# Layer 0 of a two-layer encoder trunk: row-normed inputs, evacuation on ScalarE, the residual as transposing matmuls, rotation tables as outer products

## The chip, the cores and the metric

One core of a Trainium2 chip runs the whole program. The metric is the device time of one execution in microseconds (us); the median of several runs is given.

## What is computed

Two sequences (512 and 256 tokens, each with 16 meta tokens ahead: 528 + 272 = 800 columns) go through two layers:

```python
h = concat(meta, x)                                  # 800 tokens x 1024 features
for l in range(2):
    hn = rms_norm(h, norm_mix[l])
    xa, ga, xq, xi, xff, xfb, xg, xu = split(hn @ w_in[l])
    ya = rglru(xa, ga)                               # 384 wide: conv, gates, scan both ways, gelu gate
    yb = hgrn2(silu(xq), xi, xff, xfb) * silu(xg)    # 384 wide: chunked decay attention, both ways
    yc = s5(xu)                                      # 256 wide: state space scan both ways, gelu, glu
    ym = concat(rms_norm(ya), rms_norm(yb), rms_norm(yc)) * mix_gain[l]
    h = h + ym @ w_out[l]
    h = h + relu(rms_norm(h, norm_mlp[l]) @ w_up[l])**2 @ w_down[l]
y = rms_norm(h[:, 16:], norm_final)
```

## The kernel before

Features lie on the partitions, the 800 tokens along the free dimension. A large product splits both operands into two float32r parts and runs three passes, x high by w high (L434), x low by w high (L435) and x high by w low (L436), for each of 8 (or 3, or 2) tiles of 128 input features, and for the tokens in two halves of 400. One half of one output tile fills one PSUM bank of the pool `mm`, which has three; `hb` has three and `rb` two, for everything else. Weights arrive as raw tiles `wr` (three buffers), ScalarE rounds them to `wh` (L419) and GpSimd takes the rest `wl` (L420).

A scheduler lays out the order of each engine at build time from priorities; `ORDERS` lists the steps of the mixing part of a layer (`ri`, `rc`: RG-LRU, `hi`, `hc`: HGRN2, `si`, `sc`: S5, one per tile of 128 features; `sf`: the glu of S5; `gr`, `gh`, `gw`, `hf`: smaller steps; `fB`, `fA`, `fC`: `finish`, the normed operands of `w_out` of the HGRN2, RG-LRU and S5 groups). Each engine runs its list in order, SyncE (SP), which issues the loads, too.

The functions that the change touches:

- `load` (L275) brings in seven tiles of rows of the input, sums their squares (ScalarE, L305), transposes them on TensorE (L313), rounds them to operands `xh` (ScalarE, L317) and `xl` (VectorE, L318), and copies them as the residual `h` (L319), which goes to DRAM. The rows are not normed; 1/rms of each token becomes a tile `r1` by matmuls (L306).
- Evacuations of `w_in`'s products therefore multiply by `r1` on VectorE: `scaled` (L464), `rglru_in` (L488). `hgrn_in` then takes a tanh of all 800 tokens on ScalarE (L549).
- `s5_setup` (L706) builds the tables of S5 in DRAM, for layer 0 beside the first steps, for layer 1 beside layer 0's MLP. For four sets (direction, group of four) the rotation table of 4 x 100 complex numbers is doubled seven times, six VectorE operations (L726 to L731) each: lengths 1, 2, 4, ... 64, then 36.
- `s5` (L879) handles a feature tile in four blocks: loads (L901 to L907), matmuls (L913), scans, matmuls (L940, L943) and at the end transposes (L950). `s5_glu` (L955) runs eight matmuls (L966).
- `finish` (L993), with `LT` = 1 for layer 0: the group that comes first (fB) is scaled before the product, the second (fA) and third (fC) after it.
- `mix_out` (L1066) runs `w_out` in three parts for layer 0, one per group (fB: 3 input tiles, fA: 3, fC: 2), 16 halves each. Part 0 adds the residual, loaded back from DRAM (L1091), as it leaves PSUM (L1095); parts 1 and 2 multiply (L1098) and add (L1099).
- `mlp` (L1104): evacuations of `w_up` are a relu on ScalarE (L1123) and a product on VectorE (L1124).

Of the kernel before, what the change touches and what calls it, by code (L numbers as in the profile page):

```python
# [24 lines left out]
D = 1024  # L25
# [18 lines left out]
# order in which the parts of a layer's mixers are issued  # L44
# [4 lines left out]
HALVES = ((0, 400, 0), (400, 400, 400))  # L49
HALVES_LAST = ((16, 512, 0), (544, 256, 512))  # L50
# [12 lines left out]
# per layer: what is moved in the issue order, pools of SBUF in their order, tiles of rs, hd, hs and ra, parts that  # L63
# take their tiles elsewhere, outputs that stay on chip, groups merged in w_out's first pass, engines
# [3 lines left out]
IO, PAD = ['x', 'm', 'p', 'h', 't'], 5600  # L68
# [5 lines left out]
AP = [0, 0]  # L74

class Trunk:
# [52 lines left out]
    def setup(self):  # L129
# [16 lines left out]
        # level masks: the highest bit in which s and t differ  # L146
# [12 lines left out]
        # scores of a chunk pair, block-diagonal: the blocks beside the diagonal stay zero  # L159
# [4 lines left out]
        # what leaves the chip for a while  # L164
# [19 lines left out]
        # s5 skip gains: (g2 h) rows, (l gp) columns  # L184
# [6 lines left out]
        # s5 step sizes over the states  # L191
# [9 lines left out]
        # lower bounds: softmax over the depth, running sum less the first  # L201
# [13 lines left out]
        # forget gate = hA*t + hB, key/2 = -hK*t + hK, with t = tanh(x/2)  # L215
# [6 lines left out]
        # rg-lru: softplus(-lambda) with log1p by its atanh series  # L222
# [23 lines left out]
    def gate_weights(self, l):  # L246
        """Block-diagonal gates: (i, d, r|i)."""
# [27 lines left out]
    def load(self):  # L275
        """The residual and the operands of the first w_in, half by half of the tokens."""
        nc = self.nc
        src = [(self.ins["meta_tokens"], 16)]
        src += [(self.ins["x_prompt"][0, i * 128 : i * 128 + 128], 128) for i in range(4)]
        src += [(self.ins["x_sample"][0, i * 128 : i * 128 + 128], 128) for i in range(2)]  # L280
        xs = []
        for a, n in src:
# [7 lines left out]
        h = [self.t("h") for _ in range(KD)]  # L290
        self.x = [(self._t(self.op, (128, T), F32R, f"xh{k}", 1), self._t(self.op, (128, T), F32R, f"xl{k}", 1)) for k in range(KD)]
        stat = [self.ps("hb") for _ in range(2)]
        sq = self.c((128, 8), "sq")
        for b, parts in enumerate(((0, 1, 2, 3), (4, 0, 5, 6))):
            sl = slice(b * 400, b * 400 + 400)
            # the tokens' sums of squares, from the partitions to the free dimension
# [3 lines left out]
            o = 0  # L300
            for i in parts:
                x, n = xs[i]
                if b == 0 or i:
                    junk = self.t("m", (n, D))
                    nc.scalar.activation(junk[:], x[:], AF.Square, accum_out=sq[0:n, i : i + 1])  # L305
                nc.tensor.matmul(stat[b][:, o : o + n], ap(sq[0:n], i, [[0, 128]]), self.ident[0:n, 0:n], start=True, stop=True)  # L306
                o += n
            for k in range(KD):
# [63 lines left out]
    def split(self, k, y, gain, rs=None, n=T):  # L372
        """Operand k = y*gain (*rs) as two float32r parts that add up to it exactly."""
# [12 lines left out]
    def sumsq(self, ys, n=T):  # L386
        """The sum of squares over the partitions of all tiles, on every partition: two PSUM halves."""
# [38 lines left out]
    def product(self, w, xs, halves, evac):  # L426
# [14 lines left out]
    def fetch(self, name, l, c):  # L441
        """128 columns of a weight matrix of 1024 rows, split."""
# [8 lines left out]
    def project(self, l, cols, evacs):  # L451
        """Columns of w_in, 128 from each of cols."""
# [24 lines left out]
    def rglru_in(self, l, i):  # L477
# [7 lines left out]
        def ev(b, ps):  # L485
            for c0, n in (((0, 400),), ((400, 128), (528, 272)))[b]:
                o = c0 + (2 if c0 < 528 else 5)
                nc.vector.tensor_tensor(out=xp[:, o : o + n], in0=ps[:, c0 - 400 * b : c0 - 400 * b + n], in1=self.r1[:, c0 : c0 + n], op=MULT)  # L488
# [53 lines left out]
    def hgrn_in(self, l, i):  # L542
        nc = self.nc
        FP, K2, Q, V = self.t("hd", (128, 2, T)), self.t("hd", (128, 2, T)), self.s(), self.s()
        self.project(l, (XFF + 128 * i, XFB + 128 * i), [self.scaled(K2[:, d]) for d in range(2)])
        for d in range(2):
            c = (d * 2 + l) * 3 + i
            col = lambda x: x[:, c : c + 1]
            nc.scalar.activation(K2[:, d], K2[:, d], AF.Tanh, scale=0.5)  # L549
            nc.vector.tensor_scalar(out=FP[:, d], in0=K2[:, d], scalar1=col(self.hA), scalar2=col(self.hB), op0=MULT, op1=ADD)  # L550
            nc.vector.tensor_scalar(out=K2[:, d], in0=K2[:, d], scalar1=col(self.hN), scalar2=col(self.hK), op0=MULT, op1=ADD)
        tq = self.s()
        self.project(l, (XQ + 128 * i, XI + 128 * i), (self.scaled(Q), self.scaled(V)))
        nc.scalar.activation(tq[:], Q[:], AF.Tanh, scale=0.5)
        nc.vector.scalar_tensor_tensor(out=Q[:], in0=tq[:], scalar=1.0, in1=Q[:], op0=ADD, op1=MULT)
# [18 lines left out]
    def scores(self, K, Q, P, Pm, m):  # L574
        """Scores [s, t] of level m, chunk by chunk, into the places where it applies."""
# [659 lines left out]
```

## Time and profile before

| | us |
|---|---|
| median of 3 runs (lowest to highest) | 2202.79 (2199.93 to 2209.05) |
| profiled execution: its span, first to last instruction | 2201.6 |
| TensorE matmuls busy (PE) | 2087.4 |
| VectorE busy (DVE) | 1118.9 |
| ScalarE busy (ACT) | 753.8 |
| GpSimd busy (POOL) | 811.9 |

The profiled execution has no time of its own beside its span. The page names engines PE (TensorE matmuls), PEld (weight loads), DVE, ACT, POOL (GpSimd) and SP (SyncE). Times inside the program are us from its start. PEclk is the granted clock of TensorE, 1.00 being its full speed. Layer 0's mixing part runs from 0 to about 557 us, its MLP to about 1190 us.

### The profile page before, as it was taken

Reading aid. Unit: us, or ns where it says so; the run is one execution under the profiler, and the core shown is the slowest. Engines: PE = TensorE matmul, PEld = TensorE weight load, DVE = VectorE, ACT = ScalarE, POOL = GpSimd, SP = SyncE. Lnnn points to the kernel's source line nnn. Section 1 sums busy time; section 2 is a strip of 40 time slices with the busy share of each in tenths; the row PEclk is TensorE's granted clock in tenths of the full one; section 3 lists DMA queues with packets and bytes.
Section 4 is the critical chain, followed back from the end, with each engine's and each line's share of the span. In section 5 each row is a group of like instructions: output and inputs, shape, how many; then the busy total and the mean of one; then the engine's idle time right before and its main releaser. Section 6 shows DMA issues by size and latency. Waiting matters only on the chain.

```text
span 2201.6 us, 34495 instructions
## 1 busy us (share of the span) xinstructions
PE 2087.4 (95%) x14082; PEld 1957.7 (89%) x14082; DVE 1118.9 (51%) x2258; ACT 753.8 (34%) x1141; POOL 811.9 (37%) x622
## 2 busy tenths in 40 slices
PE   8899899889989899999999999998998999999998
PEld 6889897677979899999998879886888999999997
DVE  6884748487657871221155855746368221112224
ACT  6233535454322232212225553436432122222222
POOL 1672112263433443333444213322434343434343
PEclk9899899899999999999999999998999999999998
DMA  5322111342211431122122113221321112122221
GB/s 182 96 81 76 38 40 56 101 129 57 68 48 58 109 119 58 58 64 61 58 95 78 57 37 97 74 59 48 113 79 58 58 58 68 59 67 65 60 67 68
DMA packets 230886, 160.74 MB, mean 73 GB/s; under 512 B 33270, under 2 KB 217784, under 8 KB 230728
## 3 DMA queue, kind: packets, MB, share of 16 engines
q1 hardware_dynamic: 229832, 156.95, 23.8%
q8 instruction: 111, 1.82, 0.4%
q10 hardware_dynamic: 896, 1.58, 0.2%
q14 instruction: 47, 0.39, 0.1%
HBM read 131.32 MB, written 27.18 MB: 72 GB/s over the span
## 4 chain that ended last, share of the span: by engine, by line
PE 60%; DVE 10%; ACT 2%; issue 1%; POOL 1%; DMA 1%; SPq 0%; DVEq 0%; POOLq 0%; ACTq 0%
PE mm L435 18%; PE mm L434 18%; PE mm L436 18%; PE hb L664 2%; PE hb L582 1%; DVE m L1163 1%; DVE h L1172 1%; PE rb L510 1%; DVE xl L379 1%; DVE m L1164 1%; DVE h L1154 1%; DVE r L1173 0%; DVE m L1124 0%; PE rb L862 0%; POOL wl L420 0%
## 5 line engine op out<-in xcount | busy, mean ns | idle before, releaser
L420 POOL TENSOR_TENSOR wl<-wr,wh 128x1024 fp32r<-128x1024 f32 (+3 forms) x214 | 479.3, 2240 | 1005.5 <-ACT wh L419 982.7
L434 PE MATMUL mm<-xh,wh 128*128 128x400 f32 (+3 forms) x2016 | 710.2, 354 | 33.1 <-DVE m L1124 11.1
L435 PE MATMUL mm<-xl,wh 128*128 128x400 f32 (+3 forms) x2016 | 713.9, 355 | 6.0 <-POOL xl L383 2.9
L436 PE MATMUL mm<-xh,wl 128*128 128x400 f32 (+3 forms) x2016 | 701.1, 349 | 0.7 <-POOL wl L420 0.5
L419 ACT ACTIVATE wh<-wr 128x1024 fp32r<-128x1024 f32 (+3 forms) x214 | 205.7, 962 | 764.9 <-PE mm L435 658.5
L434 PEld LDWEIGHTS mm<-xh,wh 128*128 128x128 f32 x2016 | 388.6, 193 | 52.7 <-DVE m L1124 14.1
L435 PEld LDWEIGHTS mm<-xl,wh 128*128 128x128 f32 x2016 | 389.1, 193 | 18.5 <-DVE xl L379 4.1
L436 PEld LDWEIGHTS mm<-xh,wl 128*128 128x128 f32 x2016 | 388.8, 193 | 8.9 <-POOL wl L420 0.9
L434 PE MATMUL mm<-u,wh 128*128 128x400 f32 (+1 forms) x1024 | 349.1, 341 | 6.2 <-DVE m L1124 6.2
L435 PE MATMUL mm<-u,wh 128*128 128x400 f32 (+1 forms) x1024 | 349.6, 341 | 0.0
L436 PE MATMUL mm<-u,wl 128*128 128x400 f32 (+1 forms) x1024 | 348.3, 340 | 0.0
L1150 DVE TENSOR_TENSOR h<-mm,h 128x400 f32<-128x400 f32 (+1 forms) x256 | 144.5, 565 | 331.2 <-PE mm L436 331.2
L1124 DVE TENSOR_TENSOR m<-m,mm 128x400 f32<-128x400 f32 (+1 forms) x128 | 71.1, 559 | 369.2 <-ACT m L1123 369.2
L434 PEld LDWEIGHTS mm<-u,wh 128*128 128x128 f32 x1024 | 193.3, 189 | 7.8 <-DVE m L1124 7.1
L435 PEld LDWEIGHTS mm<-u,wh 128*128 128x128 f32 x1024 | 193.2, 189 | 0.1
L436 PEld LDWEIGHTS mm<-u,wl 128*128 128x128 f32 x1024 | 193.1, 189 | 0.1
L1129 POOL TENSOR_TENSOR u<-m,u 128x800 fp32r<-128x800 f32 (+1 forms) x64 | 127.3, 1990 | 53.5 <-ACT u L1128 45.4
L1123 ACT ACTIVATE m<-mm 128x400 f32<-128x400 f32 (+1 forms) x128 | 62.3, 489 | 129.9 <-PE mm L436 115.8
L582 PE MATMUL hb<-hs,hs 64*64 64x64 f32 x2016 | 85.7, 236 | 8.8 <-ACT hs L615 5.6
L582 PEld LDWEIGHTS hb<-hs,hs 64*64 64x64 f32 x2016 | 72.2, 146 | 24.5 <-issue 11.4
L1128 ACT ACTIVATE u<-m 128x800 fp32r<-128x800 f32 (+1 forms) x64 | 55.1, 861 | 83.1 <-DVE m L1124 73.2
L616 DVE TENSOR_TENSOR hd<-hd,hd 128x800 f32<-128x800 f32 (+2 forms) x48 | 43.1, 902 | 13.3 <-ACT hs L614 12.8
(365 smaller groups left out, 2245.8 us busy)
## 6 DMA issues: line engine op xcount, KB each, us to landing
wr<-in_w_up_dram SPq DMA_DIRECT2D x64, 512.0 KB
wr<-in_w_down_dram SPq DMA_DIRECT2D x64, 512.0 KB
wr<-in_w_in_dram SPq DMA_DIRECT2D x46, 512.0 KB
h<-h SPq DMA_DIRECT2D x16, 400.0 KB
wr<-in_w_out_dram SPq DMA_DIRECT2D x32, 192.0 KB
TB<-t SPq DMA_DIRECT2D x24, 200.0 KB
F<-t SPq DMA_DIRECT2D x16, 256.0 KB
E<-t SPq DMA_DIRECT2D x16, 256.0 KB
```

Source lines behind the costliest of these rows:

```text
L419: self.nc.scalar.activation(hi[:], raw, AF.Copy)
L420: self.nc.gpsimd.tensor_tensor(out=lo[:], in0=raw, in1=hi[:].bitcast(F32), op=SUB)
L434: nc.tensor.matmul(ps[:, 0:n], wh, xh[:, c0 : c0 + n], start=(k == 0), stop=False)
L435: nc.tensor.matmul(ps[:, 0:n], wh, xl[:, c0 : c0 + n], start=False, stop=False)
L436: nc.tensor.matmul(ps[:, 0:n], wl, xh[:, c0 : c0 + n], start=False, stop=(k == last))
L582: nc.tensor.matmul(ps[c % 2 * 64 : c % 2 * 64 + 64, c // 2 * 64 : c // 2 * 64 + 64], K[hr, c0 : c0 + 64], Q[hr, c0 : c0 + 64], start=True, ...
L664: mm = lambda out, w, x: nc.tensor.matmul(out, w, x, start=False, stop=False, skip_group_check=True)
L1123: nc.scalar.activation(t[:, sl], ps, AF.Relu)
L1124: nc.vector.tensor_tensor(out=t[:, sl], in0=t[:, sl], in1=ps, op=MULT)
L1128: nc.scalar.activation(u[:, 0], t[:], AF.Copy)
L1129: nc.gpsimd.tensor_tensor(out=u[:, 1], in0=t[:], in1=u[:, 0].bitcast(F32), op=SUB)
L1150: mark = nc.vector.tensor_tensor(out=t[:, sl], in0=ps, in1=t[:, sl], op=ADD)
```

## The change

1. `load`, layer 0: ScalarE takes 1/rms of the rows themselves (Ln and Exp on a small tile) and scales the rows before the transposes. No tile `r1`, no residual copies, no residual in DRAM for layer 0.
2. So layer 0's evacuations need no factor: `scaled` and `rglru_in` become ScalarE copies, `hgrn_in` takes its tanh from PSUM by halves, and a new `silu` takes its tanh on ScalarE and its product on VectorE from PSUM by halves.
3. `finish` and `mix_out`: only the last group is scaled after its product; the middle part's evacuation is one add.
4. `mix_out`, layer 0, part 0: rows of the input are loaded again, seven DMAs of 512 columns for each four output tiles, and multiplied by the identity into the same PSUM bank after the first matmul of each half (64 matmuls); ScalarE copies the sum out.
5. `s5_setup`, both layers: powers of the rotation (8 and 13 of them) are built once for all, and each of the four tables is their outer product, six operations of 128x416 in place of 42.

```diff
-IO, PAD = ['x', 'm', 'p', 'h', 't'], 5600
+IO, PAD = ['x', 'm', 'p', 't'], 12000
...
     def load(self):
...
+            r = sq[:, new[0] : new[-1] + 1]
+            nc.scalar.activation(r, r, AF.Ln, scale=1.0 / D, bias=self.consts["eps"][:])
+            nc.scalar.activation(r, r, AF.Exp, scale=-0.5)
+            for i in new:
+                x, n = xs[i]
+                nc.scalar.activation(x[:], x[:], AF.Copy, scale=sq[0:n, i : i + 1])
...
-                (nc.vector.tensor_copy, nc.scalar.copy)[b](h[k][:, sl], ps[:, 0:400])
-        self.r1 = self._t(self.op, (128, T), F32, "r1", 1)
-        self.rstd([x[:, 0:400] for x in stat], 1.0 / D, "eps", out=self.r1)
-        for k in range(KD):
-            nc.sync.dma_start(self.hdr[k][:], h[k][:])
...
     def product(self, w, xs, halves, evac, extra=None):
...
                 nc.tensor.matmul(ps[:, 0:n], wh, xh[:, c0 : c0 + n], start=(k == 0), stop=False)
+                if extra and k == 0:
+                    extra(b, ps)
...
     def scaled(self, out):
...
+            if self.normed:
+                self.nc.scalar.activation(out[:, sl], ps, AF.Copy)
+                return
             self.nc.vector.tensor_tensor(out=out[:, sl], in0=ps, in1=self.r1[:, sl], op=MULT)
...
+    def silu(self, out):
+        t = self.s()
...
+            if self.normed or b == 1:
+                sl = sl if self.normed else slice(0, T)
+                x = ps if self.normed else out[:]
+                self.nc.scalar.activation(t[:, sl], x, AF.Tanh, scale=0.5)
+                self.nc.vector.scalar_tensor_tensor(out=out[:, sl], in0=t[:, sl], scalar=1.0, in1=x, op0=ADD, op1=MULT)
...
     def s5_setup(self, l):
...
-                while n < NCH:
-                    m = min(n, NCH - n)
-                    cmul([x[:, :, n : n + m] for x in tb], [x[:, :, 0:m] for x in tb], [x[:, ds].unsqueeze(2).to_broadcast([128, 4, m]) for x in pw[n]],
...
+                cmul([x[:] for x in tb], [P8[:, i, ds].unsqueeze(3).to_broadcast([128, 4, 13, 8]) for i in range(2)], [P1[:, i, ds].unsqueeze(2).to_broadcast([128, 4, 13, 8]) for i in range(2)],
...
         def finish(k0, nk, ctx):
...
-                late = len(self.groups) >= LT[l]
+                late = len(self.groups) == 2
...
     def mix_out(self, l):
...
+                if first and not l and m % 4 == 0:
+                    xs = []
+                    for a, w in self.tokens():
+                        xs.append((self.t("t", (w, 512)), w))
+                        nc.sync.dma_start(xs[-1][0][:], a[:, m * 128 : m * 128 + 512])
+                if first and l:
...
+                    elif first:
+                        nc.scalar.activation(t[:, o : o + w], ps, AF.Copy)
+                    elif r is None:
+                        nc.vector.tensor_tensor(out=t[:, o : o + w], in0=ps, in1=t[:, o : o + w], op=ADD)
...
+                def input_rows(b, ps, m=m % 4, xs=xs):
+                    o = 0
+                    for i in TOKENS[b]:
+                        x, w = xs[i]
+                        nc.tensor.matmul(ps[:, o : o + w], x[:, m * 128 : m * 128 + 128], self.ident[0:w, 0:w], start=False, stop=False, skip_group_check=True)
+                        o += w
```

The order of the engines' lists shifts as well. First place: TensorE's list where part 0 of `w_out` begins, beside the last RG-LRU step (L510, after the change L532) and S5's second tile (L913 to L943, after it L936 to L966). Before:

```order
L434 MATMUL mm_4885<-xh_644_4503,wh_4878 128x400
L434 MATMUL mm_4896<-xh_644_4503,wh_4878 128x400
L434 MATMUL mm_4916<-xh_644_4503,wh_4909 128x400
L510 MATMUL rb_4448<-rs_4420,gw_1144 128x402
L435 MATMUL mm_4885<-xl_645_4504,wh_4878 128x400
L436 MATMUL mm_4885<-xh_644_4503,wl_4879 128x400
L435 MATMUL mm_4896<-xl_645_4504,wh_4878 128x400
L436 MATMUL mm_4896<-xh_644_4503,wl_4879 128x400
L435 MATMUL mm_4916<-xl_645_4504,wh_4909 128x400
L436 MATMUL mm_4916<-xh_644_4503,wl_4910 128x400
```

And of the change:

```order
L433 MATMUL mm_4749<-xh_640_4352,wh_4730 128x400
L433 MATMUL mm_4764<-xh_640_4352,wh_4730 128x400
L433 MATMUL mm_4786<-xh_640_4352,wh_4781 128x400
L532 MATMUL rb_4297<-rs_4269,gw_999 128x402
L532 MATMUL rb_4300<-rs_4269,gw_999 128x401
L936 MATMUL hb_4433<-hs_4420 64x100 x8
L963 MATMUL hb_4461<-hs_4421,hs_4420 100x128
L963 MATMUL hb_4469<-hs_4421,hs_4420 100x128
L922 MATMUL hb_4480<-ident_82,hs_4402 128x100 x2
L532 MATMUL rb_4303<-rs_4269,gw_999 128x402
```

Before, the first three products go on between the other steps; now each stands with its first matmul alone in one of the three `mm` banks. Second place: the same list 40 rows on, from the transposes that end S5's second tile (L973) over the glu (L989) to the first matmuls on the input's rows (L1139):

```order
L973 MATMUL hb_4655<-ident_82,hs_4419 128x100 x4
L989 MATMUL hb_4669<-rs_3575,hs_4666 128x400
L989 MATMUL hb_4673<-rs_3575,hs_4666 128x400
L989 MATMUL hb_4678<-rs_3575,hs_4666 128x400
L989 MATMUL hb_4669<-hs_4648,hs_4666 128x400
L989 MATMUL hb_4673<-hs_4648,hs_4666 128x400
L989 MATMUL hb_4678<-hs_4648,hs_4666 128x400
L989 MATMUL hb_4682<-rs_3575,hs_4666 128x400
L989 MATMUL hb_4682<-hs_4648,hs_4666 128x400
L1139 MATMUL mm_4749<-ident_82,t_4735 128x16
L1139 MATMUL mm_4786<-ident_82,t_4735 128x16
L1139 MATMUL mm_4749<-ident_82,t_4737 128x128
```

Between the two places the list holds nothing of `w_out`; its second matmul comes after the glu. Before, 32 halves of `w_out` (parts 0 and 1) are spread from the first place to behind the glu. Third place: SyncE's list, where the rows are loaded (`t`, L1116), behind the last block of S5's loads (L924 to L930) and the glu's weights (L981):

```order
L930 DMA hs_4592<-W_38_153 128x1x128 x2
L981 DMA hs_4666<-in_s_glu_w_dram 128x2x256
L1116 DMA t_4735<-in_meta_tokens_dram 16x512
L1116 DMA t_4737<-in_x_prompt_dram 128x512
L1116 DMA t_4739<-in_x_prompt_dram 128x512
L1116 DMA t_4741<-in_x_prompt_dram 128x512
```

Before, the residual's loads stood ahead of that tile's loads and between them:

```order
L1091 DMA m_4976<-h_23_141 128x800
L1001 DMA hs_4483<-y_31_149 128x800
L1001 DMA hs_4485<-y_32_150 128x800
L1082 DMA wr_5000<-in_w_out_dram 128x3x128
L901 DMA hs_4568<-E_36_154 128x2x256
L902 DMA hs_4570<-TB_39_157 128x600
```

The rows' tiles `t` lie where tiles `rs` of the mixing part lie, those that `rc2`, `fA` and S5's first tile still use.

## Rows read from the trace of the kernel before

**Rows 1.** The page's first part: busy us, share of span, instructions.

```profile
PE 2087.4 (95%) x14082; PEld 1957.7 (89%) x14082; DVE 1118.9 (51%) x2258; ACT 753.8 (34%) x1141; POOL 811.9 (37%) x622
```

**Rows 2.** Stretches: length, busy us and instructions of each engine, PEclk, DMA share, GB/s.

```profile
50.00:75.00 25.00, 19.91 (x93) 19.23 (x92) 22.77 (x110) 6.85 (x7) 7.82 (x3) 0.86 0.39 107
100.00:150.00 50.00, 46.05 (x592) 40.36 (x593) 47.32 (x97) 18.36 (x37) 42.69 (x45) 0.97 0.28 86
150.00:200.00 50.00, 50.00 (x358) 46.08 (x355) 32.09 (x56) 17.84 (x28) 20.44 (x20) 1.00 0.27 83
435.00:490.00 55.00, 47.25 (x274) 39.46 (x275) 45.14 (x59) 36.08 (x60) 31.72 (x42) 0.94 0.42 132
700.00:800.00 100.00, 91.28 (x493) 86.75 (x492) 89.96 (x308) 24.08 (x44) 40.26 (x24) 0.93 0.39 109
800.00:1000.00 200.00, 200.00 (x1105) 198.98 (x1104) 49.25 (x88) 44.23 (x60) 74.81 (x34) 1.00 0.22 67
1190.00:1700.00 510.00, 483.63 (x3988) 425.40 (x3986) 318.64 (x496) 226.83 (x353) 157.93 (x154) 0.96 0.23 67
```

**Rows 3.** TensorE's timeline: start, duration, instruction; end of S5's second tile.

```profile
507.94 0.85 PE L950 MATMUL hb<-ident,hs 100*128 100x100 f32 x8
508.57 0.43 PE L434 MATMUL mm<-xh,wh 128*128 128x400 f32 x1
```

**Rows 4.** Lines L913, L943, L966: durations lowest/median/highest, first and last start.

```profile
L913 PE MATMUL hb<-hs x64: 249/249/302, 445.3 to 493.3; 128*64 128x100 f32 x64
L943 PE MATMUL hb<-hs,hs x64: 269/269/350, 457.4 to 503.8; 64*100 64x128 f32 x64
L966 PE MATMUL hb<-hs,hs x8: 498/499/499, 518.5 to 524.6; 128*128 128x400 f32 x8
```

**Rows 5.** VectorE's and then TensorE's timeline where part 2 and the MLP begin.

```profile
535.18 1.54 DVE L1098 TENSOR_TENSOR m<-mm,r 128x400 f32<-128x400 f32 x3 [6.28 <-ACT r L413]
...
556.49 0.67 PE L434 MATMUL mm<-xh,wh 128*128 128x400 f32 x1 [2.35 <-DVE m L1098]
556.96 0.54 PE L435 MATMUL mm<-xl,wh 128*128 128x400 f32 x1
557.29 0.54 PE L436 MATMUL mm<-xh,wl 128*128 128x400 f32 x1
```

**Rows 6.** Groups, 0 to 435 us and 435 to 557 us: busy, mean ns.

```profile
L464 DVE TENSOR_TENSOR hs<-mm,r 128x400 f32<-128x400 f32 x14 | 7.9, 567 | 12.3 <-PE mm L436 12.3
L319 DVE COPY h<-mm 128x400 f32<-128x400 f32 x8 | 4.5, 563 | 0.0
L305 ACT ACTIVATE m<-x 128x1024 f32<-128x1024 f32 x6 | 6.3, 1055 | 1.2 <-DMA x<-in_x_prompt_dram 1.2
L1095 DVE TENSOR_TENSOR h<-mm,m 128x400 f32<-128x400 f32 x16 | 8.7, 563 | 0.1
```

**Rows 7.** Waits of TensorE, 0 to 435 us and 557 to 800 us: us, times, longest.

```profile
PE mm L434 <- DVE t L731: 4.4, 1, 4.4
PE hb L582 <- ACT hs L615: 5.6, 2, 3.8
PE mm L434 <- DVE m L1124: 13.3, 4, 4.6
```

**Rows 8.** VectorE's and GpSimd's timelines around 53 us and 706 us.

```profile
53.53 2.36 DVE L727 TENSOR_TENSOR t<-t,t 128x16 f32<-128x16 f32 x1
...
58.20 0.56 DVE L464 TENSOR_TENSOR hd<-mm,r 128x400 f32<-128x400 f32 x1
...
53.50 4.69 POOL L420 TENSOR_TENSOR wl<-wr,wh 128x1024 fp32r<-128x1024 f32 x2 [5.16 <-ACT wh L419]
...
705.86 2.40 DVE L728 TENSOR_TENSOR t<-t,t 128x8 f32<-128x8 f32 x1
```

**Rows 9.** ScalarE's timeline at the start.

```profile
8.84 1.54 ACT L317 ACTIVATE xh<-mm,pc 128x400 fp32r<-128x400 f32 x3
...
11.34 1.28 ACT L412 ACT_TABLE_LOAD   x1
```

More of the change, by code (lines that the diff above doesn't have):

```diff
@@ L49 @@
 HALVES = ((0, 400, 0), (400, 400, 400))
+TOKENS = ((0, 1, 2, 3), (4, 0, 5, 6))
 HALVES_LAST = ((16, 512, 0), (544, 256, 512))
@@ L289, in load @@
         gain = self.pc["norm_mix"]
-        h = [self.t("h") for _ in range(KD)]
         self.x = [(self._t(self.op, (128, T), F32R, f"xh{k}", 1), self._t(self.op, (128, T), F32R, f"xl{k}", 1)) for k in range(KD)]
-        stat = [self.ps("hb") for _ in range(2)]
         sq = self.c((128, 8), "sq")
-        for b, parts in enumerate(((0, 1, 2, 3), (4, 0, 5, 6))):
+        nc.vector.memset(sq[:], 1.0)
+        for b, parts in enumerate(TOKENS):
             sl = slice(b * 400, b * 400 + 400)
+            new = [i for i in parts if b == 0 or i]
             if b == 1:
@@ L299, in load @@
                     self.params()
-            o = 0
-            for i in parts:
+            for i in new:
                 x, n = xs[i]
[L303 to L307, printed above, removed]
+                junk = self.t("m", (n, D))
+                nc.scalar.activation(junk[:], x[:], AF.Square, accum_out=sq[0:n, i : i + 1])
+            r = sq[:, new[0] : new[-1] + 1]
+            nc.scalar.activation(r, r, AF.Ln, scale=1.0 / D, bias=self.consts["eps"][:])
+            nc.scalar.activation(r, r, AF.Exp, scale=-0.5)
+            for i in new:
+                x, n = xs[i]
+                nc.scalar.activation(x[:], x[:], AF.Copy, scale=sq[0:n, i : i + 1])
             for k in range(KD):
@@ L424, in raw, with product @@
         return self._t(self.wp, shape, F32, "wr", 3)
-    def product(self, w, xs, halves, evac):
+    def product(self, w, xs, halves, evac, extra=None):
         nc = self.nc
@@ L487, in ev @@
                 o = c0 + (2 if c0 < 528 else 5)
-                nc.vector.tensor_tensor(out=xp[:, o : o + n], in0=ps[:, c0 - 400 * b : c0 - 400 * b + n], in1=self.r1[:, c0 : c0 + n], op=MULT)
+                src = ps[:, c0 - 400 * b : c0 - 400 * b + n]
+                if self.normed:
+                    nc.scalar.activation(xp[:, o : o + n], src, AF.Copy)
+                else:
+                    nc.vector.tensor_tensor(out=xp[:, o : o + n], in0=src, in1=self.r1[:, c0 : c0 + n], op=MULT)
         g = self.s()
@@ L544, in hgrn_in @@
         FP, K2, Q, V = self.t("hd", (128, 2, T)), self.t("hd", (128, 2, T)), self.s(), self.s()
-        self.project(l, (XFF + 128 * i, XFB + 128 * i), [self.scaled(K2[:, d]) for d in range(2)])
+        th = lambda d: lambda b, ps: nc.scalar.activation(K2[:, d, b * 400 : b * 400 + 400], ps, AF.Tanh, scale=0.5)
+        self.project(l, (XFF + 128 * i, XFB + 128 * i), [th(d) if self.normed else self.scaled(K2[:, d]) for d in range(2)])
         for d in range(2):
@@ L794, in s5_setup @@
         cmul([BB[:, i] for i in range(2)], [BRI[:, i] for i in range(2)], b, [t2[:, i] for i in range(2)])
+        P1, P8, tp = self.s((128, 2, 16, 8)), self.s((128, 2, 16, 13)), self.s((128, 2, 128))
+        for P, w0, w in ((P1, 1, 8), (P8, 8, 13)):
+            v.memset(P[:, 0, :, 0:1], 1.0)
+            v.memset(P[:, 1, :, 0:1], 0.0)
+            for i in range(2):
+                v.tensor_copy(P[:, i, :, 1], pw[w0][i])
+            n = 2
+            while n < w:
+                m = min(n, w - n)
+                cmul([P[:, i, :, n : n + m] for i in range(2)], [P[:, i, :, 0:m] for i in range(2)], [x.unsqueeze(2).to_broadcast([128, 16, m]) for x in pw[w0 * n]],
+                     [tp[:, i, 0 : 16 * m].rearrange("p (a b) -> p a b", b=m) for i in range(2)])
+                n *= 2
         for d in range(2):
@@ L987, in mix @@
         self.gate_weights(l)
+        self.normed = l == 0
         hc = lambda: self.using("hs", "hb")
@@ L1073, in mix_out @@
             first = runs is parts[0]
-            r = self.groups[-1 if runs is parts[-1] else 1][1]
-            add = nc.gpsimd if AP[l] and runs is parts[1] and len(parts) == 3 else nc.vector
+            r = self.groups[2][1] if runs is parts[-1] else None
             ks = [k for k0, w in runs for k in range(k0, k0 + w)]
@@ L1091, in mix_out, with ev @@
                         nc.sync.dma_start(res[:, o : o + w], self.hdr[m][:, c0 : c0 + w])
-                def ev(b, ps, t=new[m], res=res, first=first, r=r, add=add):
+                def ev(b, ps, t=new[m], first=first, r=r):
                     c0, w, o = halves[b]
-                    if first:
+                    if first and l:
                         nc.vector.tensor_tensor(out=t[:, o : o + w], in0=ps, in1=res[:, o : o + w], op=ADD)
+                    elif first:
+                        nc.scalar.activation(t[:, o : o + w], ps, AF.Copy)
+                    elif r is None:
+                        nc.vector.tensor_tensor(out=t[:, o : o + w], in0=ps, in1=t[:, o : o + w], op=ADD)
                     else:
@@ L1098, in ev @@
                         nc.vector.tensor_tensor(out=q[:], in0=ps, in1=r[:, c0 : c0 + w], op=MULT)
-                        add.tensor_tensor(out=t[:, o : o + w], in0=q[:], in1=t[:, o : o + w], op=ADD)
-                self.product([(hi[:, k], lo[:, k]) for k in range(nk)], [self.x[k] for k in ks], halves, ev)
+                        nc.vector.tensor_tensor(out=t[:, o : o + w], in0=q[:], in1=t[:, o : o + w], op=ADD)
+                def input_rows(b, ps, m=m % 4, xs=xs):
[4 more added lines that the diff above has]
+                        o += w
+                self.product([(hi[:, k], lo[:, k]) for k in range(nk)], [self.x[k] for k in ks], halves, ev, input_rows if first and not l else None)
         return new
```

49 lines of the change are left out of this document (22 added, 27 removed).

## Prediction

> **What bounds the kernel now.** I read the page's busy times first: TensorE is busy 2087.4 of 2201.6 us [rows 1], so an engine other than TensorE can give only what TensorE now loses to waits and to its lower clock. The stretches show where that is. From 800 to 1000 us, in the MLP, TensorE is busy all 200 us at granted clock 1.00, 1105 matmuls, 0.181 us each [rows 2]; nothing done on VectorE or ScalarE can shorten that. Losses lie in layer 0's mixing part and in the MLP's first third: 19.91 of 25 us busy at clock 0.86 from 50 to 75 us, with VectorE busy 22.77; 91.28 of 100 at clock 0.93 from 700 to 800 us, with VectorE busy 89.96 [rows 2]. In 150 to 200 us TensorE loses nothing [rows 2]. TensorE's waits say for whom: VectorE's setup operations and its evacuations [rows 7].
>
> The second thing to see is how S5's second tile is covered today. Its matmuls run from 445.3 to 508.8 us [rows 3, 4], a chain of small matmuls, scans and DMAs with long gaps. TensorE is still busy 47.25 of 55 us from 435 to 490 [rows 2], because products of `w_out` stand between. Its list holds 32 halves of parts 0 and 1 there, 9 matmuls of 0.181 us each, 26.1 us a part.
>
> **The change part by part.** The sum is made against the profiled span of 2201.6 us; the median of the runs shown is 1.2 us more, a difference I leave out.
>
> *`w_out` behind S5 (the largest term).* In the new list the first three halves of part 0 each issue one matmul, then hold all three `mm` banks, and the next thing they need, the input's rows, comes after the glu on TensorE and behind S5's last loads on SP. So parts 0 and 1 no longer cover S5. What this costs:
> - S5's tile alone. The last of its four blocks takes 493.3 to 503.8, 10.5 us from last L913 to last L943 [rows 4]; four of these from 445.3, with 0.7 for the L913 of the block, and the 4.1 us from 503.8 to the transposes at 507.9 [rows 3, 4], end at about 494. Today it ends at 508.6 [rows 3]. SP's loads of that tile stand behind the residual's in the old list, so some of the 14 us comes back. I take 501, about the middle, since the tile's other loads and scans stay as they are.
> - The glu: L966 today runs from some 10 us after the transposes (518.5) to 525.1 [rows 4]. Eight at once, with the gelu ahead: 12.5 us after them, so 513.5.
> - Part 0: 26.1 us, and 64 matmuls on the rows. Eight float32 transposes of 100 columns take 0.63 us [rows 3], so 0.1 each for 128: 6.4. TensorE has idled, so I add 3 us for a lower clock: after its wait before 556.49 the pitch is 0.33 for 0.18 [rows 5], some 20 matmuls of that. To 549.
> - Part 1: 26.1, to 575. Its evacuation is one add where there were two operations of 0.57 us, and with ScalarE's copies in part 0 VectorE is free; both are covered.
> - Part 2: as now, from 535.18 (first L1098) to 556.49 (the MLP's first product), 21.3 us [rows 5]. Its 1/rms is ready about 10 us after the glu today (525.1 to 535.2) and now lies under part 1. To 596.5.
>
> The MLP starts at 556.5 today: **+40 us**. Lower bound: S5 at 494 (−7) and part 2 at TensorE's own rate, 16 × 6 × 0.181 = 17.4 (−4), so +29. Upper: S5 no faster, 508.6 (+8), so +48.
>
> *Rows normed first.* Today ScalarE writes the first `xh` at 8.84. Ahead of it come now two table loads of 1.28 [rows 9] and four scalings like L305's 1.06 [rows 6]: some 7 us later. But the products wait for the second half's operands and for VectorE, so I take 2 us late, bounds 0 and +7. L319's 8 copies (4.5 us [rows 6]) leave VectorE.
>
> *Evacuations on ScalarE.* 49 multiplications of up to 0.567 us [rows 6], some 26 us, leave VectorE. ScalarE was under 40% busy in the early stretches shown [rows 2]. What it is worth: the evacuation at 58.20 came 4.4 us late for TensorE, behind two setup operations stalled 2.36 and 2.31 us [rows 7, 8]; on ScalarE it would not be: −4.4, and about −3 for the lower clock after the wait. HGRN2's steps wait for L615's tiles (5.6 us [rows 7]), which come from VectorE's list; fewer operations in it bring some −8 with the later steps' shorter waits. With the 2 us late, **−14 in all** before S5's second tile. Bounds: 0, as the stretch that follows can be TensorE's own, and −30, which is about the 26 us of evacuations and the 4.5 of copies handed back one for one.
>
> *Scaling fA before the product* moves two VectorE operations ahead of S5's end; they lie beside the S5 chain and cost nothing here. *The residual* in DRAM: 16 loads and stores fewer, 14 loads of rows more; loads of 256 KB that are behind the glu's on SP are on the chip before 513.5, if issued at some 0.5 us each. If they come 5 us later, the sum is 5 more; within the upper bound.
>
> *Rotation tables.* In layer 0 they are part of the relief above. In layer 1's setup, which runs on VectorE in layer 0's MLP, 168 small operations become 24 of 128x416 and about 38 that build powers. TensorE waits 13.3 us for L1124 there [rows 7], and its clock falls to 0.93 between 700 and 800 [rows 2]: 4 more. I take **−8**; bounds 0 and −13. Four evacuations still stand behind some 30 setup operations.
>
> There is a rule against this gain. At 53.53 an operation of 128x16 on VectorE takes 2.36 us while GpSimd runs L420, from 53.50; at 705.86 one of 128x8 takes 2.40 [rows 8]. So it is GpSimd's operation that sets the stall, not the size of VectorE's own.
> The Trainium skill, "SBUF — State Buffer", section "Who interferes with whom", says that the port pair of these two engines is locked for a whole instruction and that an operation of VectorE with two inputs in SBUF waits until GpSimd's is done. By this, stalls go with the count of L420 and L1129, which the change leaves alone; the term would be near 0 and the sum +26. The trace agrees with the rule where rows 8 show it.
>
> *Layer 1's mixing part* loses 26 of 510 us [rows 2]; its operations are the same in another order. I take 0, ±8.
>
> Sum: +40 −14 −8 = +18, so **2219.6 us**, say 2220.
>
> **Rivals.**
> 1. *The relief is handed back in full* (faster). The front gives −30, S5's tile runs at its own pace, part 2 at TensorE's: +29 −30 −13 = −14, so 2188. For it: VectorE busy 47.32 of 50 us from 100 to 150 [rows 2]. Against: from 150 to 200 TensorE has no idle time to give back [rows 2].
> 2. *Gains and loss cancel*: front −25, S5 +33, tables −8, so about 2202. It needs S5's tile to end near 495 and the HGRN2 steps to be VectorE's alone.
> 3. *The front gains nothing* (slower still): the copies queue on ScalarE behind the weights' roundings (L419), HGRN2's small steps and table loads, and hold the three `mm` banks as VectorE did. It decides if ScalarE's queue is as late as VectorE's was. +40 +2 −8 = +34: 2236.
> 4. *The tables do nothing*, as the stalls are GpSimd's: +26, 2228.
> 5. *The change doesn't cost what the list says*: if TensorE found `w_out` work during S5's tile after all, the first term would fall to the 6.4 us of added matmuls and the time to 2201.6 + 6.4 − 22 = 2186. The list excludes it unless TensorE leaves its order; I count it in rival 1.
>
> **How the numbers follow.** Forecast 0.41, rival 1 (with 5) 0.13, rival 2 0.23, rival 3 0.17, rival 4 0.06. A change of about 0.5%, 11 us, is what a measurement of this kernel can tell; so faster is below 2191.8, slower above 2213.8. Faster: rival 1, 0.13. Same: rival 2, 0.23. Slower: the others, 0.64. The range leaves out the best of rival 1 and what lies beyond rival 3: 2190 to 2240. The likeliest case's own range is 2209 (S5 at 494) to 2232.
>
> **What would show it.** Right: between the last RG-LRU matmuls and the glu, TensorE is mostly idle and its granted clock low; the products of parts 0 and 1 stand in one block behind the glu; the MLP begins at 575 to 590; S5's second tile takes under 56 us; the wait for the MLP's evacuation is below 13 us; the first product begins after 20 us. Wrong: the MLP begins before 557, or `w_out` matmuls stand between L936 and L989, or the first 430 us are no shorter than now.

## The result and the profile after

The changed kernel takes 2280.8 us (median of 4 runs, 2277.05 to 2281.95) beside 2204.61 before (4 runs too): a ratio of 1.0348, 95% interval 1.0323 to 1.0372. The forecast was 2220, the range 2190 to 2240. The sign was right and the size was not: the profiled span grew by 73.7 us, from 2201.6 to 2275.3, four times the 18 that were forecast. First the page's head and its busy times, of the changed kernel:

```profile
span 2275.3 us, 34452 instructions
...
PE 2114.2 (93%) x14194; PEld 1983.8 (87%) x14194; DVE 1073.9 (47%) x1984; ACT 781.2 (34%) x1200; POOL 806.9 (35%) x589
```

Beside [rows 1]: VectorE has 45 us less to do and 274 operations fewer, as the change says, and TensorE 27 us more. The time got longer all the same. Stretches of the changed kernel, columns as in [rows 2]:

```profile
100.00:150.00 50.00, 43.34 (x489) 38.61 (x488) 42.25 (x80) 18.46 (x38) 33.38 (x30) 0.90 0.24 75
400.00:447.00 47.00, 38.99 (x246) 32.22 (x247) 17.21 (x36) 15.93 (x32) 8.67 (x22) 0.60 0.11 33
447.00:525.00 78.00, 42.91 (x211) 28.28 (x209) 46.05 (x54) 41.72 (x72) 34.61 (x52) 0.67 0.27 84
525.00:571.00 46.00, 46.00 (x277) 42.26 (x277) 3.10 (x3) 18.66 (x33) 9.00 (x8) 1.00 0.29 77
571.00:597.00 26.00, 26.00 (x145) 26.00 (x144) 8.63 (x16) 4.38 (x10) 7.84 (x8) 1.00 0.18 51
762.00:862.00 100.00, 92.09 (x517) 86.99 (x516) 85.94 (x204) 25.82 (x46) 41.90 (x25) 0.98 0.39 112
1230.00:1660.00 430.00, 401.10 (x3522) 352.27 (x3521) 251.97 (x423) 203.54 (x316) 120.99 (x137) 0.95 0.22 66
```

The MLP begins 62 us later than before, so its first third is read at 762 to 862, where rows 2 have 700 to 800. S5's second tile and the glu (447 to 525) now run alone: 211 matmuls in 78 us at clock 0.67, where 274 stood in 55 us [rows 2]. Behind it parts 0 and 1 of `w_out` stand dense, 46 and 26 us. TensorE's timeline of the changed kernel at these seams:

```profile
516.24 3.55 PE L989 MATMUL hb<-rs,hs 128*128 128x400 f32 x6
521.40 2.28 PE L989 MATMUL hb<-hs,hs 128*128 128x400 f32 x6 [1.60 <-DVE hs L492]
...
524.95 1.93 PE L1139 MATMUL mm<-ident,t 16*128 16x16 f32 x14
...
528.17 0.38 PE L1139 MATMUL mm<-ident,t 128*128 128x128 f32 x2
528.31 0.43 PE L436 MATMUL mm<-xl,wh 128*128 128x400 f32 x1
...
529.85 1.34 PE L1139 MATMUL mm<-ident,t 128*128 128x128 f32 x8
530.95 0.43 PE L436 MATMUL mm<-xl,wh 128*128 128x400 f32 x1
...
618.54 0.67 PE L433 MATMUL mm<-xh,wh 128*128 128x400 f32 x1 [2.61 <-DVE m L1132]
```

The MLP's first product begins at 618.54, at 556.49 before [rows 5]: +62. The start is late too. ScalarE's timeline, then TensorE's, of the changed kernel:

```profile
9.01 1.28 ACT L301 ACT_TABLE_LOAD   x1
...
10.62 1.28 ACT L302 ACT_TABLE_LOAD   x1
...
12.97 4.25 ACT L305 ACTIVATE x<-x,sq 16x1024 f32<-16x1024 f32 x4
...
19.45 1.52 ACT L315 ACTIVATE xh<-mm,pc 128x400 fp32r<-128x400 f32 x3
```

```profile
32.37 0.70 PE L433 MATMUL mm<-xh,wh 128*128 128x400 f32 x1
```

The first operand comes at 19.45 (8.84 before [rows 9]), the first product at 32.37. TensorE's waits of the changed kernel, from 0 to 150 us and from 620 to 862 us:

```profile
PE mm L311 <- ACT x L305: 11.2, 2, 10.6
...
PE mm L433 <- DVE m L1165: 12.3, 4, 4.9
```

For the runs below the same marks are read from the one trace of each. The first sum of squares (`total`, L404 before) closes the front, everything ahead of S5's second tile. From the sum in the MLP's norm to the next layer's is the MLP; from there to the last one of layer 1's groups is layer 1's mixing part. The median is that of all runs of a kernel; its ratio is to runs of the kernel before made beside it (medians 2202.0 to 2205.9). All in us:

| kernel | first product | first sum | glu ends | MLP's sum | MLP 0 | layer 1's mixing | median | ratio to before (95%) |
|---|---|---|---|---|---|---|---|---|
| before | 20.0 | 432.3 | 525.1 | 610.8 | 560.9 | 415.2 | 2204.6 | |
| changed | 32.4 | 446.5 | 525.1 | 672.7 | 557.4 | 430.4 | 2280.8 | 1.0348 (1.0323 to 1.0372) |
| e1, no join | 32.8 | 451.4 | 545.6 | 632.6 | 556.6 | 423.5 | 2232.6 | 1.0118 (1.005 to 1.0185) |
| e2, join in part 1 | 33.5 | 450.2 | 533.6 | 655.5 | 557.4 | 433.7 | 2266.4 | 1.0271 (1.0204 to 1.0338) |
| e3, before + join | 20.4 | 434.7 | 503.9 | 650.7 | 562.0 | 414.8 | 2247.0 | 1.0183 (1.0111 to 1.0255) |
| e4, old tables | 32.5 | 455.1 | 535.1 | 683.2 | 559.1 | 428.9 | 2294.0 | 1.0396 (1.0327 to 1.0465) |
| e5, before + tables | 20.4 | 427.2 | 525.6 | 609.6 | 557.2 | 452.2 | 2229.0 | 1.012 (1.0084 to 1.0155) |
| e6, before + parts 1 to 3 | 33.4 | 465.3 | 567.7 | 653.2 | 559.8 | 437.9 | 2261.6 | 1.0251 (1.0211 to 1.0291) |
| e7, layer 1's silu as before | 32.3 | 449.7 | 528.2 | 675.2 | 556.0 | 444.3 | 2284.4 | 1.0354 (1.0319 to 1.0389) |
| e8, copies on VectorE | 32.6 | 448.4 | 526.6 | 674.4 | 556.0 | 436.2 | 2292.7 | 1.0392 (1.0354 to 1.043) |
| e9, e5 and one priority | 20.2 | 430.7 | 529.1 | 613.5 | 557.3 | 418.6 | 2207.8 | 1.0018 (0.9995 to 1.0042) |
| e10, before + norm chain | 35.0 | 446.2 | 539.1 | 623.4 | 561.1 | 413.3 | 2213.7 | 1.005 (1.0025 to 1.0076) |
| e11, tables in layer 1 only | 20.4 | 426.4 | 519.1 | 604.8 | 557.5 | 418.4 | 2200.7 | 0.9989 (0.9962 to 1.0015) |
| e12, e11 and ri2 elsewhere | 20.1 | 428.6 | 523.4 | 606.6 | 559.3 | 419.9 | 2200.6 | 0.9979 (0.9953 to 1.0005) |

How far such marks can be trusted the table shows itself. Up to the first sum, before, e3 and e11 have the same list on TensorE, row for row, and their sums stand at 432.3, 434.7 and 426.4; the changed kernel, e1, e2 and e7 have one list there too, and stand at 446.5 to 451.4. At the MLP's sum before and e11 are 6 us apart, e5 and e9 3.9. So some 8 us between two single traces show nothing by themselves.

The 73.7 us are then +62 ahead of the MLP's sum, −3.5 in MLP 0, +15.2 in layer 1's mixing part. The 62 are about 40 by the join (e3) and 12.6 by the norm's chain (e10). Some 9 are left, and the trace shows where: from the first sum to the end of the glu e3 takes 69 us, and the changed kernel, e4, e7 and e8, which like e3 have no `w_out` beside S5 but scale fA ahead of its product, take 78 to 80. VectorE and GpSimd of the changed kernel in S5's second tile, TensorE's wait there, and the same scans in e3:

```profile
493.32 2.98 DVE L380 SCALAR_TENSOR_TENSOR rs<-rs,pc,rs 128x800 f32<-128x800 f32 x3 [4.28 <-ACT rs L412]
496.22 6.07 DVE L948 TENSOR_TENSOR_SCAN hs<-hs,hs 128x100 f32<-128x100 f32 x4
...
495.36 6.45 POOL L382 TENSOR_TENSOR xl<-rs,xh 128x800 fp32r<-128x800 f32 x3 [3.24 <-ACT xh L381]
...
PE hb L963 <- DVE hs L939: 6.4, 1, 6.4
```

```profile
480.56 1.14 DVE L934 TENSOR_TENSOR_SCAN hs<-hs,hs 128x100 f32<-128x100 f32 x4 [1.25 <-POOL hs L927]
```

VectorE waits 4.3 us for fA's 1/rms, scales fA's three tiles (L380) in 3.0, and then needs 6.1 us for four of S5's scans, which take 1.1 in e3, while GpSimd works on fA's low parts (L382). S5's next steps and TensorE wait for that. No run changes fA's scaling alone.

### The profile page after: what moved, and what is told of

Same layout as the page of the kernel before. It is cut to its first block, busy times and chain, and to the rows that moved or that the text cites. A ratio compares the mean times of both kernels' runs of the same rounds, so it can differ in the third digit from the quotient of the medians.

```text
span 2275.3 us, 34452 instructions
## 1 busy us (share of the span) xinstructions
PE 2114.2 (93%) x14194; PEld 1983.8 (87%) x14194; DVE 1073.9 (47%) x1984; ACT 781.2 (34%) x1200; POOL 806.9 (35%) x589
## 4 chain that ended last, share of the span: by engine, by line
PE 62%; DVE 11%; ACT 2%; issue 1%; POOL 1%; DMA 1%; DVEq 0%; SPq 0%; POOLq 0%; ACTq 0%
PE mm L436 18%; PE mm L433 18%; PE mm L437 18%; PE hb L685 1%; DVE m L1204 1%; PE hb L603 1%; DVE h L1213 1%; PE mm L1139 1%; DVE xl L378 1%; PE rb L532 1%; DVE m L1205 1%; DVE h L1195 1%; DVE t L748 0%; DVE r L1214 0%; DVE m L1165 0%
## 5 line engine op out<-in xcount | busy, mean ns | idle before, releaser
L1165 DVE TENSOR_TENSOR m<-m,mm 128x400 f32<-128x400 f32 (+1 forms) x128 | 71.1, 559 | 372.1 <-ACT m L1164 372.1
L603 PEld LDWEIGHTS hb<-hs,hs 64*64 64x64 f32 x2016 | 70.8, 143 | 24.9 <-issue 12.4
L685 PEld LDWEIGHTS hb<-hd,hd 64*64 64x64 f32 x576 | 42.6, 148 | 8.9 <-issue 7.4
```

The costliest lines, as they stand in the source:

```text
L603: nc.tensor.matmul(ps[c % 2 * 64 : c % 2 * 64 + 64, c // 2 * 64 : c // 2 * 64 + 64], K[hr, c0 : c0 + 64], Q[hr, c0 : c0 + 64], start=True, ...
L685: mm = lambda out, w, x: nc.tensor.matmul(out, w, x, start=False, stop=False, skip_group_check=True)
L1165: nc.vector.tensor_tensor(out=t[:, sl], in0=t[:, sl], in1=ps, op=MULT)
```

## The experiments

**The join: e1, e2, e3.** e1 drops the rows' loads and matmuls:

```diff
-                if first and not l and m % 4 == 0:
+                if 0:
...
-                self.product(..., halves, ev, input_rows if first and not l else None)
+                self.product(..., halves, ev)
```

> The changed kernel without the input's rows in part 0 of w_out: no row loads, no 64 matmuls; layer 0's residual is left out. Theory (the rows' tiles come free late, so w_out is taken off S5's second tile): the list again has w_out between S5's matmuls; the 17 us of row matmuls and some 33 us of idle and half clock go, so about 2225 us, and the MLP begins near 570. Rival (the first 440 us and S5's own tile are what became slower): little but the 17 us goes, 2255 to 2260, the MLP begins at 600.

The MLP's sum comes at 632.6 instead of 672.7, 40 us earlier: the cover is back and the row matmuls are gone. The glu ends later than with the join (545.6), since S5's tile shares TensorE with `w_out` again. The whole is 7.6 us over the 2225 that were expected. The first sum came at 451.4, so the front's loss has nothing to do with the join.

e2 moves the join to part 1 (`rows = not l and runs is parts[1]` in place of `first and not l`):

> The changed kernel with the rows joined in part 1 of w_out instead of part 0; all else the same. Theory: part 0 (26 us) lies over S5's second tile again, part 1 stays behind the glu: about 2275 - 26 = 2249 us. Rival (the matmuls on the rows themselves are the cost, wherever they stand): 2270 to 2278.

The MLP's sum comes 17 us earlier, the whole 14 us: part 0 is under S5 again, though not for its full 26 us, because the glu then ends 8.5 us later, 3.7 of them from the first sum. The place of the join matters, but 2266 lies between the theory's 2249 and the rival's 2270, nearer to the rival.

e3 puts the join into the kernel before:

> The kernel before with the join alone (rows by 64 matmuls, ScalarE copies in part 0, no residual loads); the residual copies of the load part are still made and written. Theory: the join costs by itself 33 us of lost cover and 17 us of matmuls, less some of VectorE's 9 us: about 2250 us. Rival (it is harmful only with the other parts): 2205 to 2220.

2247.0, as the theory had it. Three stretches of e3, to the end of S5's transposes, over the glu and behind it:

```profile
435.00:495.00 60.00, 32.76 (x196) 22.93 (x194) 40.27 (x52) 36.60 (x65) 28.65 (x49) 0.68 0.33 100
495.00:504.00 9.00, 7.34 (x21) 3.69 (x19) 2.98 (x3) 5.26 (x8) 0.00 (x0) 0.86 0.14 53
504.00:600.00 96.00, 92.48 (x524) 86.94 (x525) 47.42 (x69) 32.90 (x56) 25.82 (x25) 1.00 0.29 78
```

Without `w_out` beside it S5's tile and the glu end 21 us earlier than before (503.9 for 525.1), TensorE being 32.8 of 60 us busy at clock 0.68; then 52 us of parts 0 and 1 and the row matmuls follow. Net 40 us at the MLP's sum, the same as in e1 from the other side.

**The tables: e4, e5, e9, e11.** e4 is the changed kernel with the old loop of doublings:

> The changed kernel with the rotation tables by doubling as before. Theory: the tables gain 2 to 4 us in MLP 0 and nothing elsewhere: 2278 us, MLP 0 some 615 us long, layer 1's mixing part as in the changed kernel (430 us). Rival (the tables shift layer 1's order and cost there): layer 1's mixing part falls to 415 and the whole to 2264.

Both missed: the tables are worth some 13 us in the changed kernel (the intervals of the two ratios overlap). 8.6 of them lie ahead of the first sum (455.1 for 446.5, or 4 beside the latest trace with the list of the changed kernel) and 1.7 in MLP 0. The rival on layer 1 falls (428.9). e5 is the reverse, the kernel before with the new `s5_setup` alone:

> The kernel before with the outer-product tables alone. Theory: they take some 9 us from the first 430 us and 3 us from MLP 0, layer 1's mixing part stays at 415: about 2193 us. Rival (what they gave in the changed kernel was an accident of its order): 2200 to 2210.

It is slower than before by 1.2%. MLP 0 is 3.7 us shorter, as the theory has it. The first sum is 5 us earlier (9 expected), which the spread above doesn't let one tell from nothing. Then layer 1's mixing part, whose code is the same, takes 452 us. That was the least expected number of the study. Part of it is only moved: 54 more matmuls stand in that stretch, and what follows it is 7.6 us shorter than before (607.0 for 614.7). What differs there is the order of the lists. A count over the traces gives the share of TensorE's 3500 matmuls of that part that stand in the same sequence as before (line and kind of tile, longest common stretches; the expectation of e9 below has its own count, by rows of the list). Beside it the time from the sum that opens layer 1 to the program's end, which leaves out what is only shifted:

| kernels | in the same sequence | layer 1's opening sum to the end, us |
|---|---|---|
| before, e3, e9, e10, e11, e12 | 99 to 100% | 1027 to 1035 |
| changed, e1, e2, e4, e6 | 92 to 94% | 1043 to 1052 |
| e5, e7, e8 | 61 to 67% | 1054 to 1059 |

e9 tests it. It adds to e5 one number:

```diff
-PR = [..., {'sf': 400, 'rc2': -400, 'hi0': -60, 'hc2': 150}]
+PR = [..., {'sf': 400, 'rc2': -350, 'hi0': -60, 'hc2': 150}]
```

> The outer-product tables alone (2229 us before this run), with one priority of layer 1 moved (rc2 from -400 to -350), a number that leaves the order of the kernel before itself as it is; with the tables it brings layer 1's list on TensorE back close to that of before (98% of its rows in the same sequence, 77% without). Theory (the list, not the tables' work, costs layer 1): layer 1's mixing part 415 to 420 us (452 in the run of the tables alone), the whole 2191 to 2197, below the kernel before. Rival (something else of the tables slows layer 1): 440 to 452, the whole 2215 to 2229.

Layer 1's mixing part in the kernel before, in e5 and in e9, each from its own stretch:

```profile
1171.70:1586.90 415.20, 396.25 (x3502) 344.72 (x3500) 247.79 (x422) 199.51 (x314) 118.48 (x136) 0.95 0.23 68
```

```profile
1166.80:1619.00 452.20, 422.42 (x3556) 367.28 (x3556) 255.49 (x425) 201.44 (x315) 124.72 (x138) 0.91 0.22 63
```

```profile
1170.80:1589.40 418.60, 399.00 (x3502) 346.01 (x3500) 250.06 (x422) 199.66 (x314) 120.17 (x136) 0.95 0.23 68
```

34 us of the mixing part come back, 24 to the program's end (1059.2 to 1035.0), and the clock with them, 0.91 to 0.95. So the order costs them, and what follows from it, such as when tiles come free: one priority is all that was changed, and the operations are the same. The whole came to 2207.8, not 2191 to 2197. Up to the MLP's sum e9 has the list of e5, and its marks are 3.5 and 3.9 us later; the gain ahead of the first sum on which the 2191 rested is not shown, and the kernel is not faster than before.

e11 uses the outer products for layer 1's tables only, and layer 1's list is that of before, row for row:

> The outer-product tables in layer 1's setup only (it lies in layer 0's MLP); layer 0's by doubling. Layer 1's list on TensorE is then that of before. Theory: 3 to 4 us less in MLP 0 and nothing else: 2200 us, layer 1's mixing part 415. Rival: layer 1 over 430.

MLP 0 is 3.4 us shorter, layer 1 418. The whole, 2200.7, can't be told from before. Over all fourteen traces MLP 0 takes 559.1 to 562.0 us with the old tables of layer 1 and 556.0 to 559.3 with the new ones, so these 3.5 us are shown.

**Rows normed and evacuations: e6, e8, e10.** e6 has parts 1 to 3 only, with the residual by DRAM taken from the normed rows:

> The kernel before with parts 1 to 3 alone (rows normed, evacuations on ScalarE, fA scaled ahead); the residual goes by DRAM as before but is taken from the normed rows; tables by doubling. Theory (these parts cost the front some 20 us and layer 1 some 13): the first total of squares starts at 455 (432 before), layer 1's mixing part is 428 long, about 2240 us. Rival (the front's loss comes from the pools of the load phase, which here lie as before): first total at 435, 2215 to 2220.

The loss ahead of the first sum is larger than expected, 33 us, and layer 1's 23; the whole, 2261.6, is above the 2240 too, and the rival on the pools falls. e10 below explains 14 of the 33. The other 19 stay open; the changed kernel with the old tables (e4) has 9 of them. e8 keeps the rows' norm and puts the evacuations back on VectorE as copies:

```diff
-                self.nc.scalar.activation(out[:, sl], ps, AF.Copy)
+                self.nc.vector.tensor_copy(out[:, sl], ps)
```

> The changed kernel with layer 0's evacuations as copies on VectorE and tanh and products as before; rows still normed first. Theory (the late start by the row norms costs the front, not ScalarE's evacuations): first total of squares at 447 or later, 2275 to 2290 us. Rival (ScalarE's list holds the evacuations): first total at 435, about 2263 us.

First sum at 448.4, within the spread of the changed kernel's list: up to there it makes no difference that can be told on which engine the 49 evacuations stand. The whole, 2292.7, is just over the 2290 expected; the 12 us above the changed kernel lie behind the MLP's sum, where layer 1's list is another (67% in the table above). e10 takes the other half, ScalarE's chain of the row norm in the kernel before, with a factor of one:

```diff
+            nc.scalar.activation(r, sq[:, new[0] : new[-1] + 1], AF.Ln, scale=0.0, bias=self.ones[:, 0:1])
+            nc.scalar.activation(r, r, AF.Exp, scale=-0.5)
+            for i in new:
+                x, n = xs[i]
+                nc.scalar.activation(x[:], x[:], AF.Copy, scale=sr[0:n, i : i + 1])
```

> The kernel before with the row norm's chain on ScalarE (two table loads, seven scalings of the rows) at a factor of one; all evacuations, the tables, the residual as before; layer 1's list the same as before. Theory (the late first product alone lengthens the first mixing part): first product at 29 to 33, first total of squares at 443 to 455 (432 before), 2216 to 2228 us. Rival (the late start is made up by 80 us, and the loss comes from the evacuations and the new order): first total at 432 to 437, 2203 to 2208 us.

First product at 35.0, later than the 29 to 33 expected; first sum at 446.2, as late as in the changed kernel and outside the 426 to 435 of the lists without the chain; the whole, 2213.7, 11 us above before and just under the theory's 2216. The way there is odd: HGRN2's second tile ends 1 us late (314.7 for 313.9), and the delay comes back in its third tile. From the end of its scores to its last matmul, before and in e10:

```profile
380.20:418.70 38.50, 35.76 (x357) 29.01 (x356) 14.78 (x44) 9.81 (x24) 8.36 (x27) 0.88 0.26 76
```

```profile
385.70:433.70 48.00, 45.27 (x356) 37.22 (x358) 13.86 (x42) 10.07 (x25) 8.43 (x27) 0.68 0.21 62
```

Some 356 matmuls stand in either; in e10 they take 9.5 us more, at clock 0.68 for 0.88. In all eight kernels with the norm's chain at the start (changed, e1, e2, e4, e6, e7, e8, e10) this stretch is 47 to 49 us, at clock 0.65 to 0.71; in those without it 38 to 41, at 0.88 to 1.00. What ties the clock there to the start, 350 us earlier, no run shows; it stays open.

**Layer 1's silu: e7.** The changed kernel with layer 1's q and gate as before:

> The changed kernel with layer 1's q input and gate written as before (full tanh and product after both products, not inside the evacuation). Theory (that moved tanh is what shifted layer 1's order): layer 1's mixing part 415 to 418 (430 in the changed kernel), about 2265 us. Rival (any small difference ahead reshuffles it): 425 to 435, 2272 to 2285.

444: the theory falls, and the rival's 425 to 435 is passed too. Putting the tanh back does not bring the list back: it is as far from before's as in e5 (61%). So e7 can't say what the moved tanh alone does.

**A version to beat both: e12.** e11 with `'ri2': 'ra'` added to the table that says where tiles lie:

> The tables in layer 1's setup only (2201 us), and RG-LRU's third input tile (ri2) put among the tiles ra instead of rs, so that its products leave PSUM without waiting for the last gate of HGRN2. Its list has ri2's products spread through HGRN2's third tile, where the kernel before has all three mm banks held and the granted clock falls. Theory (that tail runs at half clock because no product is left to fill it): HGRN2's last stretch from the end of its scores no longer than 38 us, PEclk there above 0.90 (0.88 before from 380 to 419), first total of squares by 425, about 2190 us. Rival (the chain of small operations sets the tail, filled or not): first total at 430 to 436, 2200 to 2207.

The products do fill that stretch now (37.6 us at clock 0.91, as the theory asks), but the first sum comes at 428.6, not by 425, which can't be told from e11's 426.4. The theory's 2190 is missed, and the whole, 2200.6, is as the rival has it (2200 to 2207). At 0.9979 (0.9953 to 1.0005) it is the lowest ratio of the study, and its interval still holds 1.

## Why the prediction was wrong

Four steps failed: the front (−14, measured +14), layer 1 (0, measured +15), the scaling of fA ahead of its product (put at nothing, some 9 by the traces) and the tables (−8, measured −3.5). The join, the largest term, came out. Of the prediction's own signs the block of `w_out` behind the glu is there, but the MLP begins at 618.5 and not by 590, S5's second tile takes 69 us from 447 to the end of its transposes and not under 56, and one sign of being wrong is met: the first 430 us are longer, not shorter.

**The join: right, by luck in that two errors cancel.** The forecast was +40 us to the MLP, and e3 has 39.9 at the MLP's sum. But S5's tile was put at 501 and the glu's end at 513.5; alone it ends at 503.9 (e3), by the lower bound of 494 and a glu of 9 us. (The blocks added up there, 445.3, 42.0, 0.7 and 4.1, give 492.) And the 64 matmuls on the rows were priced at 0.1 us each, from L950's transposes [rows 3]. They are products, not transposes: the four of a half, three of 128 rows and one of 16, take 1.1 us (529.85 to 530.95 in the timeline above), 0.28 each, and part 0 took 46 us for the 36 that were worked out:

```profile
L1139 PE MATMUL mm<-ident,t 128*128 128x128 f32 (+1 forms) x128 | 20.7, 285 | 0.0
```

The group of the changed kernel has two records for each of the 64, 0.285 us each, pipelined; its busy time is 20.7. A transpose of L950 has one record. The row to take was that of a plain product, such as L306 on the same identity, which has two records as well; it was left aside for one that only looked alike. Parts 1 and 2 came out as worked out: 26 us, and 21.5 from 597.0 to 618.5.

**Rows normed first: wrong, +2 for 12.4.** The step said that the products wait for the second half's operands anyway. Before, they don't: the first product begins ahead of the second half's transposes (L313 into `rb`).

```profile
19.98 0.70 PE L434 MATMUL mm<-xh,wh 128*128 128x400 f32 x1
...
L313 PE MATMUL rb<-ident,x x32: 229/272/330, 25.9 to 46.6; 128*128 128x128 f32 x24, 16*128 16x16 f32 x8
```

Now the transposes that make the first operands (L311) wait 11.2 us for L305's scaled rows. The bound of +7 counted table loads and scalings, and left out that the rest of the chain is queued in order behind them on ScalarE: behind the four scalings come two more squares ahead of the first operand (19.45), and another ahead of the fourth. e10 shows that this chain alone costs 14 us at the first sum and 11 in all; how much of that is the late start and how much the unexplained lower clock behind 400 us is open.

**Evacuations on ScalarE: −16 for about 0.** VectorE's 26 us did go. e8 puts them back, and its first sum can't be told from the changed kernel's. The step took TensorE's waits for VectorE as due to the evacuations' place in its list. In the stretch from 100 to 150 VectorE is at 42 us for 47 and TensorE at 43 for 46, which speaks for HGRN2's small steps as what sets it; this is a reading and no run tests it. It was rival 3 in that the front gains nothing; that the front would lose 14 us no rival had.

**Scaling fA ahead: 0 for some 9.** The step held that these operations lie beside the S5 chain. In the trace they stand in VectorE's list inside S5's third block, ahead of its scans (L948), wait there for fA's 1/rms, and the scans behind them take 6.1 us for 1.1.

**The tables: −8 for −3.5.** MLP 0 is 557.4 for 560.9, in e11 557.5. The wait for L1165 is 12.3 for 13.3 [rows 7]. VectorE has a third fewer operations in the stretch that was 700 to 800, 204 for 308, but is busy 86 us for 90. Operations of VectorE over 1.5 us, from 40 to 230 us behind the MLP's sum, are 17 with 37.4 us before and 18 with 37.8 us in the changed kernel, each of them beside one of GpSimd's, of which there are 37 in both. So the small operations went and the stalls stayed, and the wait with them. The Trainium skill's rule ("SBUF — State Buffer", "Who interferes with whom"), by which the stalls go with GpSimd's operations, was the better guide to that wait.

**Layer 1: 0 for +15.** The step held that the same operations in another order cost the same, give or take 8. e5 and e9 refute that: 34 us in the mixing part, 24 to the program's end, between two orders of the same operations. That the 15 us of the changed kernel have the same cause is argued from the table of sequences; no run puts its own order back. Of the 55 us by which the forecast missed, 28 are the front (+14 for −14), 15 layer 1, some 5 MLP 0; the other 8 lie between the first sum and the MLP's (48 us for 40), where fA's scaling stands. No rival came near 2281, and the range ended at the loss of the front's gain.

## What to carry to other kernels

Where a scheduler lays out the lists, cost every change twice, by its operations and by the order that comes out of it: read the new list in all stretches, also in those that the change doesn't touch, and take a tuned order that moved for a loss until a run says otherwise. An operation moved off a busy engine is worth what waits for it, not its duration. Don't count on a late start being made up: in e10 15 us at the first product had shrunk to 1 at 314 us and were 11 in the whole. Before a mark of a few us is read as a gain, find two kernels with the same list up to it and see how far apart they are.

## What was not expected of the hardware

- The 356 matmuls of HGRN2's last stretch took 38.5 us at a mean granted clock of 0.88 and 48.0 at 0.68 (before and e10). After a stretch with gaps (TensorE 2.1 of 4 us busy from 400 to 404 in the changed kernel) the clock stayed at the lower level, 1.2 GHz, for 30.7 us though TensorE was busy throughout:

```profile
402.80:433.50 30.70, 30.70 (x190) 24.39 (x190) 6.48 (x20) 5.29 (x15) 4.56 (x19) 0.50 0.13 40
```

- Four float32 products with the identity, three of 128 columns and one of 16, so 100 on average, took 1.10 us at full clock (529.85 to 530.95), 0.28 each, where a transpose of 100 columns had a pitch of 0.08 (eight in 0.63 us [rows 3]).
- Four scans of VectorE on 128x100 took 6.07 us beside operations of GpSimd (changed kernel, 496.22) and 1.14 us with GpSimd idle but for a MEMSET of 0.14 us (e3, 480.56).
